# Gated linear attention inside a decoder layer: the coarsest level as a key-value state, two lanes of heads, tiles for pairs of heads

## The chip, the cores and the metric

One NeuronCore of a Trainium2 chip runs the whole program. The metric is the device time of one execution in microseconds; the kernel before took 889.64 us (median of 3 runs, 889.6 to 890.25). Engines are called as the profile calls them: PE is the matrix engine with its weight loads PEld, DVE the vector engine, ACT the scalar engine, POOL the general-purpose engine, SP the one that issues most loads.

## The reference

The reference is one decoder layer on 512 tokens of width 1024. A layer norm feeds one wide input projection, whose columns are split among gated linear attention (GLA, 4 heads, key width 128, value width 256), latent attention (MLA, 8 heads) and two branch gates. Both branches are projected back, merged by the gates, projected once more, normalised, and followed by a squared-ReLU MLP of width 4096. The part that is changed is GLA, which for each head computes

```
S_t = diag(a_t) S_{t-1} + k_t^T v_t
o_t = q_t S_t
```

with a decay a_t for every key channel, then a root-mean-square norm of o over its 256 columns, times silu(r), times an output projection:

```
log_a = log_sigmoid(a_lr @ w_gla_a2 + b_gla_a2) / 16
o_gla = gla_chunked(q * 128 ** -0.5, k, v, log_a)
y_gla = (rms_norm(o_gla) * silu(r_g)) @ w_o_gla
```

## The kernel before, in words

Everything is float32 in and out. Large products are made of three matmuls: each operand is split into a high part of type float32r and a low remainder (`split`, L104: one ACT copy for the high part, one DVE subtraction for the low one), and high x high, high x low and low x high are summed. Weights come through one list, `stream`; `pump` (L156) issues their loads on SP a few entries ahead and splits them (L179 on ACT, L180 on DVE) one entry ahead of their use.

**Lanes.** `gemm_tm` (tokens on the partitions) and `gemm_fm` (features on the partitions) run over the reduction in blocks of 128. After each block `tick` lets the first few generators of the list `active` (the first `WID[0]`) trace one step, up to their next `yield`. That is how small work is put between the matmuls of large products: a lane is a generator, and a step of it is what it does between two yields. A program then orders the instructions of each engine by a simulated timeline, with the order of tracing as priority.

**The stages around the change.** After the latents (`latents`, `latents2`) come the products of the input projection: queries, keys, then for each pair of heads `proj_v` and `proj_r` (values and output gates, 512 columns for two heads, 8 blocks each), then four products for the branch gates (`ev_g`, L941, tanh into the tiles `gt`) with the query-rope products `mla_qr` between them. GLA's levels and outputs run in lanes beside all of these; `finish(*t_gla)` (L972) closes the lanes ahead of `y_gla(0)`.

**Levels.** `gla_levels(h)` computes the 512x512 causal matrix of scores of a head by halves: at level s = 1, 2, 4, ..., 256 the right half of every block of 2s tokens looks at its left half, with decays taken relative to the middle. `advance` (L613, two POOL additions) keeps running sums of log decays in `rp`; `vec(s)` (L632) exponentiates them (ACT, L634) and multiplies them into queries and keys (DVE, L637 or L641) to give `M`; a matmul of the two halves of `M` gives the scores into a PSUM tile `px`; `take` (L646) puts them where they belong. Levels up to 64 go into the diagonal 128x128 blocks `SD` by a predicated copy; level 128 gives two blocks `s128`; level 256 gives, at L697, a 256x256 block of scores between the first and the last 256 tokens, as two matmuls with operands of type float32:

```
for j in range(2):
    mm(p[:, j * 256:(j + 1) * 256], M[:, j * P:(j + 1) * P], M[:, 256:], start=True, stop=True)
```

which `take` splits into `s256`. The first 256 columns of `M` are then the keys of the first half with their decays, the last 256 the queries of the last half with theirs. At the end the diagonal blocks are transposed where needed (L708) and split into `sd`. One lane, `lane_levels`, does the four heads one after the other.

**Outputs.** `gla_out(h)` waits until the levels, values and gates of its head are there, then sums for each block row i of 128 queries over its i + 1 blocks of keys (`blk`), three matmuls of 256 columns for each (L738 to L740), squares the result for the norm (L742), multiplies by the gate (`og`, L752), transposes (L758) and splits the result into `ogT` (L761). A lane of its own, `lane_out`, does this head after head.

**Buffers.** Tiles of tag A (24 buffers of 4 KB a partition) hold, among others, `latT`, `KK`, `qk`, `rp`, the values `vh` and `vl`, the gates `rg`, `sd`, `s256`, `ogT` and `gt`; tag B has 22 of 2 KB. PSUM has 4 banks for the large products (tag mm) and 4 for everything else (tag px). A tile waits until a buffer of its tag has been read for the last time. In `proj_v(1)` the evacuation is preceded by `levels_upto(1)`, which traces levels until heads 0 and 1 are through, so that their buffers are free.

Of the kernel before, what the change touches and what calls it, by code (L numbers as in the profile page):

```python
# [19 lines left out]
P = 128  # L20
# [32 lines left out]
def tile_hybrid_block(ctx: ExitStack, tc: tile.TileContext, I, out, dbg=None):  # L53
# [521 lines left out]
    Vh = [None] * GH  # L575
    Rg = [None] * GH
# [12 lines left out]
    def proj_r(hp):  # L589
        hs = (2 * hp, 2 * hp + 1)  # L590

        def e(a, j, ps):
            th = B([P, T], F32, "th")
            act(th, ps, AF.Tanh, scale=0.5)
            for i, h in enumerate(hs):
                if Rg[h] is None:
                    Rg[h] = A([P, NT, HV], F32, "rg")
                stt(Rg[h][:, a, :], th[:, i * HV:(i + 1) * HV], 1.0, ps[:, i * HV:(i + 1) * HV],
                    op0=ALU.add, op1=ALU.mult)
        gemm_tm([PL["r", hp]], hT, T, e)  # L600
# [3 lines left out]
    def gla_levels(h):  # L604
# [6 lines left out]
        s128 = s256 = None  # L611
# [34 lines left out]
        def take(s, p):  # L646
            nonlocal s128, s256
# [19 lines left out]
        advance(1)  # L667
        yield
# [16 lines left out]
        prev = None  # L685
        while s < T:
# [8 lines left out]
            else:  # L695
                for j in range(2):
                    mm(p[:, j * 256:(j + 1) * 256], M[:, j * P:(j + 1) * P], M[:, 256:], start=True, stop=True)  # L697
# [13 lines left out]
        take(*prev)  # L711
# [3 lines left out]
        SS[h] = (sd, s128, s256)  # L715
        yield

    def gla_out(h):
        while SS[h] is None or Vh[h] is None or Rg[h] is None:
            yield  # L720
        sd, s128, s256 = SS[h]

        def blk(j, i, w):
            if i == j:
                return sd[:, w, i, :]
            if j // 2 == i // 2:
                return s128[:, w, j // 2, :]
            return s256[:, w, j, (i - 2) * P:(i - 1) * P]

        vh, vl = Vh[h]  # L730
        ss = S([P, NT], F32, "gss")
        ps = []
        for i in range(NT):
# [3 lines left out]
            for j in range(i + 1):  # L737
                mm(o, blk(j, i, 0), vh[:, j, :], start=j == 0, stop=False)  # L738
                mm(o, blk(j, i, 0), vl[:, j, :], start=False, stop=False)
                mm(o, blk(j, i, 1), vh[:, j, :], start=False, stop=j == i)  # L740
# [9 lines left out]
        for i in range(NT):  # L750
            o = ps[i // 2][:, (i % 2) * HV:(i % 2 + 1) * HV]
            stt(og[i // 2][:, i % 2, :], o, rs[:, i:i + 1], Rg[h][:, i, :], op0=ALU.mult, op1=ALU.mult)  # L752
# [178 lines left out]
    t_gla = [t_lv, t_out]  # L931
# [376 lines left out]
```

## Time and profile before

| What | Value |
|---|---|
| median of 3 runs | 889.64 us (889.6 to 890.25) |
| the profiled execution | 889.94 us |
| its span, first to last instruction | 888.0 us |
| mean granted PE clock | 0.996 |
| input projection of values and gates, GLA, first branch gates | about 95 to 300 us of the span |
| HBM read, written | 82.56 MB, 3.67 MB |

Lines of the profile show a group of instructions as line, engine, operation, output tile <- input tiles, shapes, count, busy time, mean duration, and the idle time of the engine just before with what ended it. A piece of the chain has its start, its length and what it is; the chain is followed back from the last instruction, and a matmul's piece in it lasts until the next piece begins. Buffer numbers are left out of tile names, so `px` is any tile of tag px and `s` is `s128` or `s256`.

### The profile page before, as it was taken

The numbers are of one execution on the slowest core, as the hardware profiler recorded it, in microseconds if no ns is written. First come the engines' busy times: TensorE is split into PE (matmuls) and PEld (weight loads), VectorE is DVE, ScalarE is ACT, GpSimd is POOL, SyncE is SP. The second block draws the span as 40 slices with busy tenths as digits, with TensorE's granted clock in tenths as the row PEclk, the third lists the DMA queues.
The fourth block names the chain that finished last, engine by engine and source line by source line (L and its number), as shares of the span: only waits on it lengthen the run. The fifth ranks groups of instructions, "written<-read, shape, count | busy, mean of one in ns | idle before, by whom it ended". The sixth has DMA issues, their size and how long they took to land.

```text
span 888.0 us, 11561 instructions
## 1 busy us (share of the span) xinstructions
PE 866.7 (98%) x4352; PEld 738.3 (83%) x4352; DVE 578.2 (65%) x987; ACT 432.7 (49%) x734; POOL 173.8 (20%) x211
## 2 busy tenths in 40 slices
PE   5999999999999999999999999999999999999995
PEld 5988888888888888889888888988888888888884
DVE  7834875667735234657766797997557646754687
ACT  5446453445434334435654423466357546645661
POOL 0303441434512010000000012104400520242022
PEclk9999999999999999999999999999999999999998
DMA  7513223221223232111307628006940991398075
GB/s 231 147 48 90 77 72 95 72 72 48 78 59 88 74 107 91 61 46 55 102 25 277 190 70 286 1 0 158 296 117 25 258 254 31 70 308 192 1 189 95
DMA packets 63270, 101.13 MB, mean 114 GB/s; under 512 B 7761, under 2 KB 31748, under 8 KB 63216
## 3 DMA queue, kind: packets, MB, share of 16 engines
q1 hardware_dynamic: 48256, 64.04, 23.4%
q0 software_dynamic: 13040, 32.71, 15.3%
q10 hardware_dynamic: 1920, 3.66, 1.2%
q8 instruction: 34, 0.56, 0.2%
q14 instruction: 20, 0.16, 0.1%
HBM read 82.56 MB, written 3.67 MB: 97 GB/s over the span
## 4 chain that ended last, share of the span: by engine, by line
PE 95%; DVE 2%; DMA 2%; issue 1%; ACT 0%; POOLq 0%; SPq 0%; POOL 0%; DVEq 0%; ACTq 0%
PE mm L230 16%; PE mm L232 16%; PE mm L231 16%; PE mm L263 5%; PE mm L265 5%; PE mm L264 5%; PE px L1153 3%; PE px L1155 3%; PE px L1154 3%; PE mm L1153 2%; PE mm L1155 2%; PE mm L1154 2%; PE px L690 1%; DMA x<-in_x_dram 1%; PE px L852 1%; PE px L265 1%
## 5 line engine op out<-in xcount | busy, mean ns | idle before, releaser
L180 DVE TENSOR_TENSOR wlo<-wraw,whi 128x1024 fp32r<-128x1024 f32 (+1 forms) x104 | 117.4, 1129 | 152.8 <-ACT whi L179 147.6
L230 PE MATMUL mm<-h,whi 128*128 128x512 f32 x416 | 162.8, 393 | 0.0
L231 PE MATMUL mm<-h,whi 128*128 128x512 f32 x416 | 162.2, 390 | 0.0
L179 ACT ACTIVATE whi<-wraw 128x1024 fp32r<-128x1024 f32 (+1 forms) x104 | 100.2, 963 | 122.2 <-PE mm L231 62.9
L232 PE MATMUL mm<-h,wlo 128*128 128x512 f32 x416 | 155.3, 390 | 0.0
L1181 POOL DMA_DIRECT2D res<-ev x54 | 47.8, 989 | 236.2 <-ACT ev L1179 196.4
L232 PEld LDWEIGHTS mm<-h,wlo 128*128 128x128 f32 x416 | 78.1, 188 | 16.3
L230 PEld LDWEIGHTS mm<-h,whi 128*128 128x128 f32 x416 | 78.1, 188 | 15.6
L231 PEld LDWEIGHTS mm<-h,whi 128*128 128x128 f32 x416 | 78.1, 188 | 15.6
L264 PE MATMUL mm<-wlo,h 128*128 128x512 f32 x128 | 50.6, 395 | 0.0
L265 PE MATMUL mm<-whi,h 128*128 128x512 f32 x128 | 50.3, 394 | 0.0
L263 PE MATMUL mm<-whi,h 128*128 128x512 f32 x128 | 49.9, 400 | 0.0
L1235 ACT ACTIVATE relu<-mm 128x512 f32<-128x512 f32 x32 | 18.8, 595 | 57.3 <-PE mm L232 57.3
L351 POOL TENSOR_TENSOR mv<-mv,mhalf 128x1 f32<-128x1 f32 x4 | 5.5, 1385 | 209.2 <-DVE mv L350 209.2
L616 POOL TENSOR_TENSOR rp<-rp 128x256 f32<-128x256 f32 x32 | 29.9, 936 | 63.6 <-ACT E L634 52.8
L641 DVE TENSOR_TENSOR M<-E,qk 128x256 f32<-128x256 f32 x48 | 28.9, 629 | 12.4 <-ACT E L634 12.2
L634 ACT ACTIVATE E<-rp 128x512 f32<-128x512 f32 x32 | 20.4, 638 | 26.2 <-POOL rp L617 26.1
L179 ACT ACTIVATE xh<-wraw 128x1024 fp32r<-128x1024 f32 (+1 forms) x20 | 18.9, 959 | 26.9 <-PE mm L265 15.5
L180 DVE TENSOR_TENSOR wlo<-wq,whi 128x1024 fp32r<-128x1024 f32 x15 | 18.4, 1224 | 19.7 <-ACT whi L179 19.7
L265 PEld LDWEIGHTS mm<-whi,h 128*128 128x128 f32 x128 | 24.1, 188 | 4.8
L264 PEld LDWEIGHTS mm<-wlo,h 128*128 128x128 f32 x128 | 24.1, 188 | 4.5
L263 PEld LDWEIGHTS mm<-whi,h 128*128 128x128 f32 x128 | 24.0, 188 | 4.2
(381 smaller groups left out, 2235.2 us busy)
## 6 DMA issues: line engine op xcount, KB each, us to landing
wraw<-in_w_in_dram SPq DMA_DIRECT2D x40, 512.0 KB, 3.7
wraw<-in_w_ff_dram SPq DMA_DIRECT2D x32, 512.0 KB, 8.0
wq<-in_w_ff_dram POOLq DMA_DIRECT2D x32, 512.0 KB, 9.3
res<-ev POOLq DMA_DIRECT2D x54, 256.0 KB, 8.8
wraw<-in_w_o_gla_dram SPq DMA_DIRECT2D x8, 512.0 KB, 3.7
wraw<-in_w_o_mla_dram SPq DMA_DIRECT2D x8, 512.0 KB, 3.3
wraw<-in_w_out_dram SPq DMA_DIRECT2D x8, 512.0 KB, 4.2
wraw<-in_w_in_dram SPq DMA_DIRECT2D x8, 360.0 KB, 4.6
```

Source lines behind the costliest of these rows:

```text
L179: st["ins"] = act(hi[:, :nk, :n], raw[:, :nk, :n], AF.Copy)
L180: vtt(lo[:, :nk, :n], raw[:, :nk, :n], f(hi[:, :nk, :n]), op=ALU.subtract)
L230: mm(o, hi[:, c], xh, start=first, stop=False)
L231: mm(o, hi[:, c], xl, start=False, stop=False)
L232: mm(o, lo[:, c], xh, start=False, stop=last)
L263: mm(o, xh, hi[:, :n], start=opens, stop=False, skip_group_check=share)
L264: mm(o, xh, lo[:, :n], start=False, stop=False, skip_group_check=share)
L265: mm(o, xl, hi[:, :n], start=False, stop=last, skip_group_check=share)
L1153: mm(o, xh[:, c], hi[:, pp, cols], start=opens, stop=False, skip_group_check=True)
L1154: mm(o, xh[:, c], lo[:, pp, cols], start=False, stop=False, skip_group_check=True)
L1155: mm(o, xl[:, c], hi[:, pp, cols], start=False, stop=hf == 1 and pp == 1, skip_group_check=True)
L1181: nc.gpsimd.dma_start(res[tt + t][:, j * T:(j + 1) * T], e, accum_op=ALU.add)
```

## The change

Four things are changed, all in GLA.

1. Level 256 no longer makes scores. The keys' half of `M` is transposed on PE (two 128x128 transposes into `px`) and split into `kq[:, 0]`; the queries' half is split into `kq[:, 1]`. `gla_out` multiplies the transposed keys with the values of the first 256 tokens, which gives a state of 128x256 (6 matmuls), splits it into `sh` and `sl`, and for the block rows 2 and 3 multiplies the queries with this state, in place of two blocks of scores with their values.
2. Two lanes, `lane_levels(0)` and `lane_levels(1)`, do heads 0 and 2, and heads 1 and 3; the second starts one step later. Each level is two steps in place of one (matmul with the next level's `vec`, then `take`), with one more yield at the start and one after the first level. `WID[0]` is 4 in place of 3.
3. Values are split, and gates are made, in tiles of 2 token blocks x 512 columns for a pair of heads (`Vp`, `Rp`), in place of 4 blocks x 256 columns for each head (`Vh`, `Rg`); the number and the size of the tiles are the same.
4. `levels_upto(h)` steps the two lanes in turn.

```diff
     def proj_v(hp, guard=None):
-        hs = (2 * hp, 2 * hp + 1)
+        vp = []
         def e(a, j, ps):
-            for i, h in enumerate(hs):
-                if Vh[h] is None:
-                    Vh[h] = (A([P, NT, HV], F32R, "vh"), A([P, NT, HV], F32R, "vl"))
-                split(ps[:, i * HV:(i + 1) * HV], Vh[h][0][:, a, :], Vh[h][1][:, a, :])
+            if a % 2 == 0:
+                vp.append((A([P, 2, T], F32R, "vh"), A([P, 2, T], F32R, "vl")))
+            split(ps, vp[-1][0][:, a % 2, :], vp[-1][1][:, a % 2, :])
+            if a == NT - 1:
+                Vp[hp] = vp
...
     def proj_r(hp):
...
-            for i, h in enumerate(hs):
-                if Rg[h] is None:
-                    Rg[h] = A([P, NT, HV], F32, "rg")
-                stt(Rg[h][:, a, :], th[:, i * HV:(i + 1) * HV], 1.0, ps[:, i * HV:(i + 1) * HV],
-                    op0=ALU.add, op1=ALU.mult)
+            if a % 2 == 0:
+                rg.append(A([P, 2, T], F32, "rg"))
+            stt(rg[-1][:, a % 2, :], th, 1.0, ps, op0=ALU.add, op1=ALU.mult)
+            if a == NT - 1:
+                Rp[hp] = rg
...
         def take(s, p):
...
-                s256 = A([P, 2, 2, 2 * P], F32R, "s256")
-                split(p.rearrange("p (a b) -> p a b", b=256), s256[:, 0], s256[:, 1])
+                split(p[:, :256], kq[:, 0, 0], kq[:, 0, 1])
...
         advance(1)
         yield
+        yield
...
-        prev = None
+        yield
         while s < T:
...
                 for j in range(2):
-                    mm(p[:, j * 256:(j + 1) * 256], M[:, j * P:(j + 1) * P], M[:, 256:], start=True, stop=True)
-            if prev is not None:
-                take(*prev)
-            prev = (s, p)
+                    nc.tensor.transpose(p[:, j * P:(j + 1) * P], M[:, j * P:(j + 1) * P], ident)
+                kq = A([P, 2, 2, 256], F32R, "kq")
+                split(M[:, 256:], kq[:, 1, 0], kq[:, 1, 1])
+            if 2 * s < T:
+                M = vec(2 * s)
+            yield
+            take(s, p)
             s *= 2
             if s < T:
-                M = vec(s)
-            yield
+                yield
...
     def gla_out(h):
...
+        def V(j):
+            c = slice(h % 2 * HV, (h % 2 + 1) * HV)
+            return [t[:, j % 2, c] for t in Vp[h // 2][j // 2]]
+        p = PX()[:, :HV]
+        for j in range(2):
+            vh, vl = V(j)
+            kh, kl = [kq[:, 0, w, j * P:(j + 1) * P] for w in range(2)]
+            mm(p, kh, vh, start=j == 0, stop=False)
+            mm(p, kh, vl, start=False, stop=False)
+            mm(p, kl, vh, start=False, stop=j == 1)
+        sh, sl = B([P, HV], F32R, "gst"), B([P, HV], F32R, "gst")
+        split(p, sh, sl)
...
-            for j in range(i + 1):
-                mm(o, blk(j, i, 0), vh[:, j, :], start=j == 0, stop=False)
-                mm(o, blk(j, i, 0), vl[:, j, :], start=False, stop=False)
-                mm(o, blk(j, i, 1), vh[:, j, :], start=False, stop=j == i)
+            todo = [(sd[:, 0, i, :], sd[:, 1, i, :], *V(i))]
+            if i % 2:
+                todo.append((s128[:, 0, i // 2, :], s128[:, 1, i // 2, :], *V(i - 1)))
+            if i > 1:
+                c = slice((i - 2) * P, (i - 1) * P)
+                todo.append((kq[:, 1, 0, c], kq[:, 1, 1, c], sh, sl))
+            for n, (ah, al, bh, bl) in enumerate(todo):
+                mm(o, ah, bh, start=n == 0, stop=False)
+                mm(o, ah, bl, start=False, stop=False)
+                mm(o, al, bh, start=False, stop=n == len(todo) - 1)
...
-    def lane_levels():
-        for o in range(2):
-            nc.vector.tensor_copy(lmask[:, :, o], lmi[:, o, :, None, :].to_broadcast([P, len(LEVELS), 2, 64]))
-        for h in range(GH):
+    def lane_levels(first):
+        if first == 0:
+            for o in range(2):
+                nc.vector.tensor_copy(lmask[:, :, o], lmi[:, o, :, None, :].to_broadcast([P, len(LEVELS), 2, 64]))
+        else:
+            yield
+        for h in range(first, GH, 2):
             yield from gla_levels(h)
             lv[h] = True
...
-    t_lv, t_out = spawn(lane_levels()), spawn(lane_out())
+    t_lv, t_out = [spawn(lane_levels(first)) for first in range(2)], spawn(lane_out())
     def levels_upto(h):
-        while not lv[h]:
-            step(t_lv)
-    WID[0] = 3
+        for g in range(h + 1):
+            while not lv[g]:
+                step(t_lv[g % 2])
+    WID[0] = 4
```

More of the change, by code (lines that the diff above doesn't have):

```diff
@@ L610, in gla_levels @@
         SD = B([P, NT, P], F32, "SD")
-        s128 = s256 = None
+        s128 = kq = None
         def advance(s):
@@ L646, in take @@
         def take(s, p):
-            nonlocal s128, s256
+            nonlocal s128, kq
             if s <= 64:
@@ L710, in gla_levels @@
         gtt(sd[:, 1, :2], SD[:, :2], f(sd[:, 0, :2]), op=ALU.subtract)
-        take(*prev)
         yield
@@ L714, in gla_levels @@
         split(pt, sd[:, 0, 2:], sd[:, 1, 2:])
-        SS[h] = (sd, s128, s256)
+        SS[h] = (sd, s128, kq)
         yield
     def gla_out(h):
-        while SS[h] is None or Vh[h] is None or Rg[h] is None:
+        while SS[h] is None or Vp[h // 2] is None or Rp[h // 2] is None:
             yield
[L721 to L730, printed above, removed]
+        sd, s128, kq = SS[h]
+        def V(j):
[10 more added lines that the diff above has]
+        split(p, sh, sl)
         ss = S([P, NT], F32, "gss")
@@ L751, in gla_out @@
             o = ps[i // 2][:, (i % 2) * HV:(i % 2 + 1) * HV]
[L752 removed]
+            stt(og[i // 2][:, i % 2, :], o, rs[:, i:i + 1], Rp[h // 2][i // 2][:, i % 2, h % 2 * HV:(h % 2 + 1) * HV],
+                op0=ALU.mult, op1=ALU.mult)
         yield
@@ L930, in tile_hybrid_block @@
     proj_r(1)
-    t_gla = [t_lv, t_out]
+    t_gla = [*t_lv, t_out]
     gt = [None] * NK
```

6 lines of the change are left out of this document (3 added, 3 removed).

## The prediction

> **What bounds the kernel now.** First the page: busy shares, then the chain that ended last.
>
> ```profile
> span 888.0 us, 11561 instructions
> ...
> PE 866.7 (98%) x4352; PEld 738.3 (83%) x4352; DVE 578.2 (65%) x987; ACT 432.7 (49%) x734; POOL 173.8 (20%) x211
> ...
> PE 95%; DVE 2%; DMA 2%; issue 1%; ACT 0%; POOLq 0%; SPq 0%; POOL 0%; DVEq 0%; ACTq 0%
> ```
>
> TensorE is busy for 98% of the span and makes up 95% of the chain. That is an average, so the next view is the busy time in the stretch where the changed code runs (the four value and gate projections and the first branch-gate products, 95 to 300 us) and in the three that follow; columns are busy time and instructions of PE, weight loads, DVE, ACT, POOL, then granted clock, DMA share, GB/s. From the list of the weight loads' waits over the whole run stands the one row of a late weight split (total, times, longest).
>
> ```profile
> 95.00:300.00 205.00, 204.95 (x1079) 175.43 (x1078) 129.54 (x245) 95.41 (x182) 70.41 (x86) 1.00 0.26 75
> 300.00:400.00 100.00, 99.49 (x510) 84.15 (x509) 46.86 (x97) 36.78 (x69) 4.01 (x4) 1.00 0.24 72
> 400.00:500.00 100.00, 99.97 (x555) 87.15 (x554) 69.59 (x172) 54.22 (x117) 0.00 (x0) 1.00 0.37 125
> 500.00:600.00 100.00, 99.65 (x545) 86.19 (x544) 89.96 (x137) 42.11 (x64) 11.33 (x12) 1.00 0.30 98
> ```
> ```profile
> PEld mm L232 <- DVE wlo L180: 0.9, 1, 0.9
> ```
>
> In the changed stretch PE stands still for 0.05 us of 205, at full clock, while DVE is busy 63% and ACT 47%. So two things decide: what the edit does to the sum of PE's own time, which falls through to the end, and whether the new order opens holes in a stream that has none. Time on ACT, DVE and POOL costs nothing until it makes PE wait. A busy PE need not be PE at its peak, so the prices come from the chain, where each piece lasts until the next begins.
>
> **The PE terms.** Pieces of heads 0 and 1 from the chain (start, us, what), then the groups of the stretch, which give the counts (busy, mean ns; that mean overlaps with its neighbours and is no price).
>
> ```profile
> 127.38 0.22 PE px L708 x2
> ```
> ```profile
> 174.76 0.86 PE px L697 x4
> 175.62 0.44 PE px L758 x4
> ...
> 180.18 0.12 PE px L738
> ```
> ```profile
> L738 PE MATMUL px<-vh,s 128*128 128x256 f32 x24 | 7.0, 293 | 0.0
> L758 PE MATMUL px<-ca,og 128*128 128x128 f32 x32 | 5.0, 272 | 0.0
> L738 PE MATMUL px<-vh,sd 128*128 128x256 f32 x16 | 4.7, 296 | 0.0
> L697 PE MATMUL px<-M 128*128 128x256 f32 x16 | 4.1, 379 | 0.0
> L708 PE MATMUL px<-ca,SD 128*128 128x128 f32 x8 | 1.5, 272 | 0.0
> ```
>
> *Removed*: the level-256 score block, two float32 matmuls of 256 columns per head at L697. They stand as 16 records for four heads, so two for each matmul: 4 records, 0.86 us per head, 3.44 us in all.
>
> *Added in its place*: two transposes of 128x128 float32 per head. Transposes show one record each (8 at L708 for four heads' two, 32 at L758 for four heads' eight), 0.22 us for two in the one row and 0.44 for four in the other. So 0.22 us per head, 0.88 in all.
>
> *Output products*: before, head h has 1+2+3+4 = 10 blocks of three matmuls of 256 columns, which is the 24 + 16 = 40 of L738 over four heads. After: three each for block rows 0 to 3 with 1, 2, 2 and 3 blocks, that is 8 blocks, and 2 more for the state, 10 again. Thirty matmuls per head at 0.12 us before and after: nothing gained, nothing lost. What looks like the point of the change, a smaller product, is an equal one here; the gain sits in the float32 scores.
>
> Sum on PE: 0.88 - 3.44 = -2.56 us. Bounds for the transposes, which run before this in other places only: by L708 and L758 0.11 each; if they cost what a float32 matmul of 128 columns does, half of an L697 matmul (0.86 / 2 / 2 = 0.215), 0.43 per head and the sum is -1.72. I take 0.11: same operation, same type, same shape as in those two rows.
>
> The Trainium skill, page "TensorE: Matmul & The Clock Gate", Part 4 (PE-mode transpose), gives about 275 ns for a transpose inside a kernel. The two groups of transposes above agree with it as a duration (272 ns), but their spacing in the chain is 0.11 us; by 275 ns each, one after the other, the estimate of the sum would be 4 x 0.55 - 3.44 = -1.24 us.
>
> **ACT and DVE.** The rows for the tiles that become wider, and for their neighbours of the other width:
>
> ```profile
> L107 DVE TENSOR_TENSOR vl<-mm,vh 128x256 fp32r<-128x256 f32 x16 | 6.0, 413 | 0.1
> L598 DVE SCALAR_TENSOR_TENSOR rg<-th,mm 128x256 f32<-128x256 f32 x16 | 5.7, 414 | 1.7 <-ACT th L594 1.7
> L107 DVE TENSOR_TENSOR s<-px,s 128x512 fp32r<-128x512 f32 x4 | 2.7, 678 | 0.0
> L106 ACT ACTIVATE vh<-mm 128x256 fp32r<-128x256 f32 x16 | 5.6, 399 | 0.4 <-PE mm L265 0.2 <-DVE vl L107 0.2
> L106 ACT ACTIVATE s<-px 128x512 fp32r<-128x512 f32 x4 | 2.5, 614 | 0.6 <-PE px L697 0.6
> ```
>
> Value and gate tiles of 512 columns: 16 x 0.413 becomes 8 x 0.678 on DVE (-1.2 us), the same for the gate product at L598 (16 x 0.414 to 8 x 0.68, -1.2), and 16 x 0.399 to 8 x 0.614 on ACT (-1.5). Level 256: one split of 512 columns per head becomes three of 256 (keys, scaled queries, state): ACT 4 x (3 x 0.399 - 0.614) = +2.3, DVE 4 x (3 x 0.413 - 0.678) = +2.2. Net +0.8 us on ACT and -0.2 on DVE over 205 us: nothing, covered by PE's stream. The state's split is the one new wait inside a chain: its two instructions (0.40 + 0.41 us) stand between the state's last matmul and the third block row's second product; the first two block rows (9 matmuls, 1.1 us) and a step of the projection lie between. No DMA is added or moved.
>
> **The two lanes.** One round of a projection is 12 matmuls of 512 columns (4 x 0.68 = 2.7 us of PE), after which every lane takes one step. These are the stations of one level:
>
> ```profile
> L641 DVE TENSOR_TENSOR M<-E,qk 128x256 f32<-128x256 f32 x48 | 28.9, 629 | 12.4 <-ACT E L634 12.2
> L634 ACT ACTIVATE E<-rp 128x512 f32<-128x512 f32 x32 | 20.4, 638 | 26.2 <-POOL rp L617 26.1
> ...
> L616 POOL TENSOR_TENSOR rp<-rp 128x256 f32<-128x256 f32 x32 | 29.9, 936 | 63.6 <-ACT E L634 52.8
> L617 POOL TENSOR_TENSOR rp<-rp 128x256 f32<-128x256 f32 x32 | 24.0, 750 | 9.7 <-ACT q L660 7.5
> ```
>
> 0.94 + 0.75 + 0.64 + 2 x 0.63 = 3.6 us for one level, against one step of 2.7 before and two (5.4) after. Each head gets slower, but two run at once. Counting yields: a head takes 12 steps before and 21 after, so four heads take 48 and then 43 (the second lane starts one later). Work per step rises by 48/43, 12%; DVE's 63% in the stretch has room. I cost it at nothing. If that cover goes, the weight split L180 is late, and PE stands.
>
> What follows the levels has slack too: the last head's transposes L758 stand at 272.73 (next fence), and the branch-gate products that must come before their use end at 319.0. In steps, the last output starts about three later than before (49 against 46, 8 us), of 46 us.
>
> **Sum.** The profiled execution took 889.94 us (span 888.0), 0.30 over the median of the runs, 889.64. 889.94 - 2.56 = 887.4, and **887.1** for the median: 0.29% faster. A measurement of this kernel tells about 0.2%, 1.78 us, from no change.
>
> **Rivals.** The rows for them: the tanh of the second branch-gate product and where it waits (ACT, in time; an execution row's last bracket is the idle time before it and its releaser), head 3's output products (PE), all of L941, and two chain pieces.
>
> ```profile
> 264.99 2.03 ACT L941 ACTIVATE gt<-mm,hbg 128x512 f32<-128x512 f32 x3
> ...
> 267.73 0.69 ACT L941 ACTIVATE gt<-mm,hbg 128x512 f32<-128x512 f32 x1 [0.40 <-PE px L740]
> ```
> ```profile
> 259.17 0.28 PE L738 MATMUL px<-vh,sd 128*128 128x256 f32 x1
> ...
> 268.12 0.28 PE L740 MATMUL px<-vh,sd 128*128 128x256 f32 x1
> ```
> ```profile
> L941 ACT ACTIVATE gt<-mm,hbg x16: 672/690/694, 238.1 to 319.0; 128x512 f32<-128x512 f32 x16
> ```
> ```profile
> 272.73 0.87 PE px L758 x8
> ...
> 323.27 1.14 DVE wlo L180
> ```
>
> *A. The buffers run out (slower).* The 24 buffers of tag A hold latents, keys, values, gates, levels' results, outputs and branch gates. Before, at the second branch-gate product, 25 are asked for (6 latents and rope keys, 3 values and gates of head 3, its 2 level results, 6 outputs, 4 + 4 branch gates), and the trace shows it: the fourth tanh sits idle for 0.40 us until an L740 product of head 3 is done. After, values and gates are held by pairs until the second head is through, and head 3's output starts later: 6 + 4 + 2 + 2 + 4 outputs + 4 + 4 = 26. Two tiles wait, and behind them ACT's queue and the two accumulators that the next gate product needs. For: the row. Against: the query-rope product (36 matmuls of 0.12 us) lies before that next product, needs other accumulators, and PE executes head 3's first block rows, which free two buffers, in it. At the second value projection the count is 24, full but not over. Price if the cover fails: head 3's products take from 259.17 to 268.24 (the last one's start + 0.12), 9.1 us with 3.6 of PE's own; PE stands for at most 5.5. Then 887.1 + 5.5 = 892.6, slower by 0.33%. It decides from 4.3 us of new standstill (2.56 + 1.78).
>
> *B. Small holes take the gain back (no measurable change).* Late weight splits: one occurs already, the 0.9 us wait on L180, which stood behind other DVE work at 323.27 and left PE idle 0.51 us between 300 and 400. With 12% denser vector work ahead of the split, one such hole at each of the four projections' ends is 4 x 0.5 = 2.0: 889.1. For: DVE is the busiest of the others. Against: evacuations get shorter by the widths above, and 0.05 us of idle in 205 leaves little sign that the queue is near its limit.
>
> *C. The transposes cost more (no measurable change).* At 272 ns in a row, the groups' mean, 4 x 2 x 0.272 = 2.18 in place of 3.44 gives -1.26: 888.4. Against it the spacing of 0.11 in both rows. At 0.215 it is 887.9, on the edge. The skill's figure on that page would give the same result, since it is the duration.
>
> *D. More than the sum.* Existing holes may close as the order shifts: 0.05 + 0.51 + 0.03 + 0.35 = 0.94 between 95 and 600. That bounds a surplus: 886.1.
>
> **Chances.** Forecast, with new holes under 0.8 us: 0.60, its own range 886.1 to 887.9. D 0.03. B 0.20, C 0.05. A 0.12. Faster is forecast and D, 0.63; same is B and C, 0.25; slower is A, 0.12. Range: from 885.9, just under D's bound, up to 890.4, which takes in C and holes of up to 3.3 us; most of A and little else is left out.
>
> **What would show it.** In the trace after: no L697-like matmul of 256 columns, and two transpose records there, 0.22 us apart from their follower; 32 records at each of the three output lines and 8 at each of the state's three; PE's busy time between 95 us and the end of the branch-gate products shorter by 2.5 us at equal idle; the tanh of gate tiles idle on an output product, by how much longer than 0.40 tells A's size. If PE shows waits of over 1 us in the list between 95 and 330, or transposes spaced at more than 0.15, the sum is wrong; if the stretch gains 2.5 us and the end does not, it was given back behind it, in the attention stage.

## The result and the profile after

The changed kernel takes **898.2 us** (median of 5 runs, 897.59 to 899.05) against 890.25 (5 runs, 889.6 to 890.9): a ratio of 1.0084, interval 1.0070 to 1.0099. It was forecast at 887.1 with 885.9 to 890.4 as the range; it became slower by 8 us. The profiled execution took 897.59 us, its span is 895.5, 7.5 more than before.

The page after, span, busy shares and the chain that ended last:

```profile
span 895.5 us, 11522 instructions
...
PE 867.9 (97%) x4344; PEld 738.6 (82%) x4344; DVE 583.3 (65%) x979; ACT 434.3 (49%) x734; POOL 169.6 (19%) x211
...
PE 90%; DVE 6%; DMA 2%; issue 1%; ACT 1%; POOLq 0%; POOL 0%; SPq 0%; DVEq 0%; ACTq 0%
```

The shares hardly moved, but DVE went from 2% to 6% of the chain. The next view is the busy time of the stretch from 95 to 300 us and of the three behind it (columns as in the prediction), then the list of what PE waited for between 95 and 330 us (total, times, longest).

```profile
95.00:300.00 205.00, 198.69 (x1038) 169.46 (x1037) 132.61 (x235) 93.33 (x177) 66.11 (x85) 0.98 0.25 72
300.00:400.00 100.00, 99.49 (x503) 83.90 (x502) 43.88 (x91) 35.98 (x67) 3.90 (x4) 1.00 0.24 71
400.00:500.00 100.00, 99.97 (x561) 87.39 (x559) 70.15 (x176) 55.52 (x122) 0.00 (x0) 1.00 0.34 113
500.00:600.00 100.00, 99.65 (x544) 86.19 (x543) 89.19 (x132) 39.79 (x58) 11.21 (x12) 1.00 0.35 116
```
```profile
PE px L691 <- DVE SD L651: 3.0, 1, 3.0
PE px L691 <- DVE M L642: 2.4, 1, 2.4
PE mm L263 <- DVE vl L107: 0.5, 1, 0.5
PE px L675 <- DVE SD L684: 0.4, 1, 0.4
```

All of the loss is in the changed stretch: PE stands for 205 - 198.69 = 6.31 us there (0.05 before), at a granted clock of 0.98, and for as long as before in the three others. Two waits of level matmuls (L691) on DVE make up 5.4 us of it (the first two rows). Here is the first, on PE, at the end of the first value projection (start, duration, instruction; in brackets the idle time before it and its releaser):

```profile
123.35 0.39 PE L265 MATMUL mm<-whi,h 128*128 128x512 f32 x1
123.58 1.50 PE L691 MATMUL px<-M 128*128 128x128 f32 x12
128.09 1.22 PE L691 MATMUL px<-M 128*128 128x128 f32 x4 [3.01 <-DVE SD L651]
129.86 0.79 PE L263 MATMUL mm<-whi,h 128*128 128x512 f32 x1 [0.55 <-DVE vl L107]
130.45 0.63 PE L264 MATMUL mm<-wlo,h 128*128 128x512 f32 x1
...
134.59 0.39 PE L265 MATMUL mm<-whi,h 128*128 128x512 f32 x1
```

The last matmul of the product starts at 123.35. Level matmuls follow that need no more than what DVE has delivered; then PE stands, and the next product cannot begin because its accumulators are still to be evacuated (L107). When it does begin, its matmuls of 512 columns have 0.63 us in place of 0.39: the clock record of the trace grants 0.5 from 127.6 to 134.4 us. What DVE, and POOL beside it, did meanwhile:

```profile
123.40 1.25 DVE L180 TENSOR_TENSOR wlo<-wraw,whi 128x1024 fp32r<-128x1024 f32 x1
124.57 3.12 DVE L642 TENSOR_TENSOR M<-E,qk 128x256 f32<-128x256 f32 x4
127.61 0.42 DVE L651 COPY_PREDICATED SD<-cmask,px 128x256 f32<-128x256 uint8 x1
127.94 1.26 DVE L642 TENSOR_TENSOR M<-E,qk 128x256 f32<-128x256 f32 x2
129.13 0.68 DVE L107 TENSOR_TENSOR vl<-mm,vh 128x512 fp32r<-128x512 f32 x1
129.73 0.74 DVE L642 TENSOR_TENSOR M<-E,qk 128x256 f32<-128x256 f32 x2
```
```profile
128.13 0.79 POOL L617 TENSOR_TENSOR rp<-rp 128x256 f32<-128x256 f32 x1
129.00 0.68 POOL L618 TENSOR_TENSOR rp<-rp 128x256 f32<-128x256 f32 x1
```

DVE has no pause: a weight split of 1.25 us, then four level products in a row (the same level of both lanes), a masked copy and two more products, and only at 129.13 the evacuation. Two more things are to be seen. DVE was late long before the hole; the chain, which before runs on PE alone between 100 and 130 us, now runs mostly on DVE there, in pieces like these:

```profile
116.22 2.32 DVE M L642 x4
...
118.80 2.45 DVE M L642 x3
```

And its products are slow while POOL adds: four take 3.12 us (0.78 each) beside POOL's additions, two take 0.74 (0.37 each) right after the last of them has ended at 129.68.

The busy time of 110 to 135 us, before and then after, says how full DVE was (the same columns):

```profile
110.00:135.00 25.00, 25.00 (x127) 21.06 (x126) 18.64 (x34) 13.17 (x27) 10.94 (x15) 1.00 0.21 64
```
```profile
110.00:135.00 25.00, 21.08 (x95) 17.38 (x94) 25.00 (x42) 10.85 (x18) 18.82 (x23) 0.86 0.15 43
```

18.64 of 25 us became 25.00 of 25, and POOL went from 10.94 to 18.82. The second hole, 2.4 us at the end of the second gate projection (215 us), has another shape: DVE had an idle moment just before it, and the product that PE waits for stands behind a weight split, one small instruction and two masked copies in DVE's order.

```profile
214.92 1.23 DVE L180 TENSOR_TENSOR wlo<-wraw,whi 128x1024 fp32r<-128x1024 f32 x1 [0.42 <-ACT whi L179]
216.06 0.61 DVE L757 TENSOR_SCALAR gss<-gss 128x4 f32<-128x4 f32 x1
216.59 0.75 DVE L651 COPY_PREDICATED SD<-cmask,px 128x256 f32<-128x256 uint8 x2
217.25 0.75 DVE L642 TENSOR_TENSOR M<-E,qk 128x256 f32<-128x256 f32 x2
217.92 2.47 DVE L598 SCALAR_TENSOR_TENSOR rg<-th,mm 128x512 f32<-128x512 f32 x4
```

So the time is accounted for: 6.26 us more of standstill, and some 2.9 us for the half clock (an estimate: in the 6.8 us of half clock PE worked 5.8, and half of that is lost; 2.2 of it because eleven matmuls of 512 columns came every 0.43 us instead of 0.23). That leaves, by difference, about 1.7 us of PE work saved: 6.3 + 2.9 - 1.7 = 7.5. What had to be settled is which part of the change opens such holes, and whether the saving is there at all.

### The profile page after: what moved, and what is told of

Its sections match the earlier page's. It is cut to its first block, busy times and chain, and to the rows that moved or that the text cites. A ratio compares the mean times of both kernels' runs of the same rounds, so it can differ in the third digit from the quotient of the medians.

```text
span 895.5 us, 11522 instructions
## 1 busy us (share of the span) xinstructions
PE 867.9 (97%) x4344; PEld 738.6 (82%) x4344; DVE 583.3 (65%) x979; ACT 434.3 (49%) x734; POOL 169.6 (19%) x211
## 4 chain that ended last, share of the span: by engine, by line
PE 90%; DVE 6%; DMA 2%; issue 1%; ACT 1%; POOLq 0%; POOL 0%; SPq 0%; DVEq 0%; ACTq 0%
PE mm L230 16%; PE mm L232 16%; PE mm L231 16%; PE mm L263 5%; PE mm L265 5%; PE mm L264 5%; PE px L1170 3%; PE px L1172 3%; PE px L1171 3%; PE mm L1172 2%; PE mm L1170 2%; PE mm L1171 2%; DVE M L642 2%; DMA x<-in_x_dram 1%; PE px L865 1%
## 5 line engine op out<-in xcount | busy, mean ns | idle before, releaser
L180 DVE TENSOR_TENSOR wlo<-wraw,whi 128x1024 fp32r<-128x1024 f32 (+1 forms) x104 | 117.7, 1133 | 158.2 <-ACT whi L179 147.5
L642 DVE TENSOR_TENSOR M<-E,qk 128x256 f32<-128x256 f32 x48 | 31.3, 693 | 1.8 <-ACT E L635 1.8
L180 DVE TENSOR_TENSOR wlo<-wq,whi 128x1024 fp32r<-128x1024 f32 x15 | 18.4, 1223 | 19.7 <-ACT whi L179 19.7
```

The lines of the kernel that those rows point to most:

```text
L180: vtt(lo[:, :nk, :n], raw[:, :nk, :n], f(hi[:, :nk, :n]), op=ALU.subtract)
L642: vtt(packed(M, s, i), pairs(E[:, 2 * i * P:2 * (i + 1) * P], s), half_lr(qk, s, i), op=ALU.mult)
```

## The experiments

Times are medians, ratios are against the kernel before on the same chip, with their interval. "Standstill" is 205 us less PE's busy time from 95 to 300 us. A "hole" is counted from the start of PE's last matmul ahead of it to the start of the next one, so it is longer than the wait in the profile's list by the 0.27 to 0.42 us of that matmul (3.28 us here for the first wait of 3.0, 2.66 for the second of 2.4). "Phase" is where the steps of the levels fall against the ends of the products.

### Each part alone

Three kernels made from the one before by one part of the diff each, and one with two parts: the key-value state (e1), the two lanes (e2), the pair tiles (e3), state and tiles in one lane (e4). The letters in the expectations name the suspects: L is the two lanes, S the state, T the tiles. The edits are those of the diff above; e1, for instance:

```diff
-                    mm(p[:, j * 256:(j + 1) * 256], M[:, j * P:(j + 1) * P], M[:, 256:], start=True, stop=True)
+                    nc.tensor.transpose(p[:, j * P:(j + 1) * P], M[:, j * P:(j + 1) * P], ident)
+                kq = A([P, 2, 2, 256], F32R, "kq")
+                split(M[:, 256:], kq[:, 1, 0], kq[:, 1, 1])
...
```

> The kernel before with the key-value state alone: one lane of levels, values and gates per head. Theory L (two lanes put more vector work into one projection than DVE can do, PE stands behind it): no holes over 1 us, the float32 scores are gone, so 2.6 us under the kernel before, between 1.6 and 3.4. Theory S (the state's transposes, splits and its wait are what costs): 4 us or more over the kernel before. Theory T (512-column evacuations are late): as L, since the tiles are not in it.

> The kernel before with the two lanes and their step structure alone: scores at level 256, values and gates per head. Theory L: the holes of the changed kernel come back without the state, so its loss without its gain, 8 + 2.6 = about 10 us over the kernel before, between 6 and 13, with a hole of 2 us or more near the end of the first value projection and PE at half clock behind it. Theories S and T: within 1.5 us of the kernel before.

> The kernel before with values and gates in tiles for pairs of heads alone. Theory T: 4 us or more over the kernel before, with DVE's low parts of the values late at the end of the first value projection. Theories L and S: within 1.5 us of the kernel before; shorter evacuations (some 1 us on each of DVE and ACT) give PE nothing, since it does not wait for them.

> The changed kernel with the lanes taken back: state and pair tiles stay, one lane, one step per level. Theory L: 2.6 us under the kernel before, between 1.6 and 3.6, as the sum of the prediction has it. Theories S and T: still over the kernel before by 3 us or more.

| kernel | us | ratio | standstill, us | holes over 2 us, at |
|---|---|---|---|---|
| e1, state | 894.92 | 1.0049 (1.0036 to 1.0062) | 4.47 | 3.06 at 211 |
| e2, lanes | 898.25 | 1.0085 (1.0072 to 1.0098) | 5.15 | 3.27 at 124, 2.08 at 128 |
| e3, tiles | 897.82 | 1.0079 (1.0067 to 1.0091) | 4.15 | 2.98 at 212 |
| e4, state and tiles | 898.75 | 1.0090 (1.0076 to 1.0103) | 6.17 | 2.33 at 206, 2.71 at 210 |

Each of the three parts alone makes the kernel slower, by 4.5 to 7.9 us (state and tiles together by 8.4), and the three losses sum to far more than the whole change lost. Theory L foretold e2, with its hole and the half clock behind it, but a gain for e1 and e4; S and T foretold the losses of e1 and e3, and T had the hole of e3 at another place. So no one part is guilty, and the price is not the price of an operation. Two shapes can be told apart. With two lanes (e2 here, from 110 to 135 us) DVE is as full as in the changed kernel:

```profile
110.00:135.00 25.00, 20.17 (x95) 17.27 (x96) 25.00 (x46) 10.53 (x21) 18.17 (x22) 0.86 0.20 56
```

With one lane DVE is hardly fuller in that stretch than before (e1 18.74, e3 19.51, e4 18.60 us, before 18.64), PE does not stand there, and the holes over 2 us are near the end of the second gate projection. In e3, which changes nothing but the tiles, DVE starts the level-256 product that PE waits for at 213.97, behind a weight split (211.51) and two output splits (212.65).

### Level matmuls held behind the product

Rival: PE's fixed order has level matmuls too early, ahead of work that it could do. f1 (the changed kernel), f2 (e4) and f10 (e1) put each of them behind the latest matmul of the large product:

```diff
-                    mm(o, xl, hi[:, :n], start=False, stop=last, skip_group_check=share)
+                    st["mm"] = mm(o, xl, hi[:, :n], start=False, stop=last, skip_group_check=share)
...
+        def lmm(op, *a, **kw):
+            with tc.issue_after(st["mm"].ins):
+                op(*a, **kw)
...
-                    mm(p[:, u * P:(u + 1) * P], M[:, 0, u, :], M[:, 1, u, :], start=True, stop=True)
+                    lmm(mm, p[:, u * P:(u + 1) * P], M[:, 0, u, :], M[:, 1, u, :], start=True, stop=True)
```

> The changed kernel with one addition: every matmul and transpose of the levels is issued on PE behind the last matmul of a large product that was traced ahead of it, so none can be put ahead of the next product's first matmuls. Theory O (PE's fixed order holds level matmuls at the end of a product, and PE stands there until DVE has made their operands): the waits of 3.0 and 2.4 us on level matmuls are gone, and the time falls from 898 to 887 to 889. Theory D (DVE itself is behind in the first projection, whatever PE's order): the wait moves to the next product's first matmul, which waits for the low part of the values, 2 us or more there, 892 to 897.

> State and pair tiles in one lane, as before, with the same addition. Theory O: the waits of 4.4 us on level matmuls near the end of the second gate projection go, 887 to 889.5. Theory D: DVE is at 60% in that stretch, so it has no say here; if the time stays over 894, theory O is wrong for one lane.

> The key-value state alone in one lane (895 without the addition), with the level matmuls behind the large product's. Theory O: the 2.8 us wait on a level matmul and its half clock go, 887 to 889.5. If it stays at 893 or more, the state itself costs.

f1 took 901.25 us (ratio 1.0124, 1.0108 to 1.0139), f2 898.31 (1.0093, 1.0079 to 1.0107), f10 896.61 (1.0070, 1.0058 to 1.0083): none better than its kernel without the edit by more than 0.5 us. The waits of PE in f1:

```profile
PE mm L263 <- DVE vl L107: 5.7, 1, 5.7
PE mm L230 <- DVE rg L598: 2.9, 1, 2.9
```

The level matmuls no longer wait at these ends, and the next product's first matmul waits in their place, for the evacuations, longer than before. At these ends it is DVE that is late, and which of PE's matmuls stands first does not help. In f2 and f10 the hold did not move the hole at all: PE still waits for level products, 4.3 us against 4.4 in e4 and 3.2 against 3.2 in e1. So for kernels with one lane these two leave the rival undecided.

### The same instructions, one empty step earlier or later

If the fixed order on DVE at the ends decides, then the phase of the level steps against the products must do so too, with no work changed. f4 is the kernel **before** with one empty step ahead of the levels:

```diff
     def lane_levels():
...
+        yield
         for h in range(GH):
             yield from gla_levels(h)
```

> The kernel before with one empty step ahead of the levels: the same instructions on every engine, every level traced one step later. Theory O says that what decides is where the levels' steps fall against the products' ends, so this alone moves the time by 2 us or more, most likely up, 892 to 898. If only added or removed work matters, it stays within 1 us of the kernel before.

900.5 us, ratio 1.0117 (1.0103 to 1.0131): 10.4 us for an empty step. PE's waits between 95 and 330 us, and the hole, which stands behind the two transposes of one head and ahead of the next head's first level:

```profile
PE px L674 <- ACT vh L106: 3.7, 1, 3.7
PE px L697 <- DVE M L637: 2.2, 1, 2.2
```
```profile
178.33 0.38 PE L708 MATMUL px<-ca,SD 128*128 128x128 f32 x2
182.45 2.90 PE L674 MATMUL px<-x,qk 128*128 128x192 f32 x8 [3.74 <-ACT vh L106]
```

In the kernel before the same two follow one another without a wait. The larger wait is put down to ACT and not to DVE. The copies L664, which the next head's first level needs, start on ACT at 180.88, behind evacuations of the values and a weight split, and in the kernel before at 177.32 (f4 first, then before):

```profile
180.88 0.45 ACT L664 ACTIVATE x<-qk 128x256 f32<-128x256 f32 x1
```
```profile
177.32 0.73 ACT L664 ACTIVATE x<-qk 128x256 f32<-128x256 f32 x2
```

So either engine's fixed order can open such a hole. This settles most of it: the kernel before sits in a phase in which no such meeting occurs, and it loses more by leaving it than the changed kernel lost. The next two move kernels that have the change, by two steps (the levels of each lane behind two empty steps):

```diff
+        for _ in range(2):
+            yield
         for h in range(first, GH, 2):
```

> The kernel before with the key-value state alone, and two empty steps ahead of the levels, which moves all of them by two rounds of a product against its end; the instructions are the same as without the empty steps (894.92 us). Theory P (the phase of the levels against the ends decides): the time differs by more than 2 us from 894.92, with the holes in other places; a phase without holes gives 887 to 888. Rival (the state itself costs time): 894 to 896 us, the hole near 211 us stays.

> The changed kernel with two empty steps ahead of each lane of levels, the instructions the same. Theory P: the time differs by more than 2 us from 898.2, holes in other places; a phase without holes gives 887 to 888. Rival (two lanes and pair tiles cost their time at any phase): 897 to 900 us with the holes at 125 and 215 us.

g2 (e1 and two steps) took 903.35 us (1.0144, 1.0129 to 1.0159), 8.4 more than e1, with a standstill of 9.53 us: four holes of 1.2 to 2.4 us between 176 and 187 us, where e1 has one of 1.4, and the one at the end of the second gate product still there, 2.44 us in place of 3.06. g4 (the changed kernel and two steps) took **891.33** (1.0014, 1.0005 to 1.0024), 6.9 less than the changed kernel, with 3.38 us of standstill and full clock in the whole stretch. The program's instructions are the same within each of the three pairs (with f4 and the kernel before); the phase is worth -7 to +10 us. DVE is full in g4 too, 10.00 of 10 us from 120 to 130, and the hole there is only 1.04 us: what counts is what stands on a full DVE at the end of a product. That a phase without any hole would be met so easily was too hopeful.

### Keeping the levels in step

f5 (the changed kernel) and f11 (e1) place each level's exponential behind the latest weight split's instruction on ACT, so that the levels cannot run ahead of the products:

```diff
-            act(pairs(E, s), lr(rp, s), AF.Exp, scale=1.0 / 16.0)
+            with tc.issue_after(st["ins"].ins):
+                act(pairs(E, s), lr(rp, s), AF.Exp, scale=1.0 / 16.0)
```

> The changed kernel, with the exponential of each level placed behind the latest weight split's instruction on ACT, so that levels keep step with the products; all work is kept. Theory D (at the end of a product the vector engine has level work in its fixed order that it ran too early or too late, and TensorE stands behind it): with levels paced there is less vector work bunched at the ends, the two holes of 3.3 and 2.7 us and the half clock after the first go, 888 to 893 us. Rival (the place of the levels in the order decides and pacing only moves it): a hole of 2.5 us or more is again at an end of a value or gate product, 895 to 901 us.

> The kernel before with the key-value state alone, and the same pacing of the levels; all work is kept. Theory D: the hole of 3.06 us at 211 us and the half clock behind it go, and the 2.56 us of TensorE show: 887 to 890 us. Rival (place decides): 893 to 898 us with a hole of 2.5 us or more at an end.

f5: 893.21 us (1.0039, 1.0021 to 1.0057). Its stretch from 110 to 135 us:

```profile
110.00:135.00 25.00, 24.66 (x125) 21.01 (x125) 20.92 (x34) 10.01 (x16) 11.43 (x13) 1.00 0.22 64
```

DVE falls from 25.00 to 20.92 us there, POOL from 18.82 to 11.43, and the first hole is gone: the third of a microsecond that is left is an earlier wait, at 110 us, which the changed kernel has too (0.4 us, the last row of its list). So that hole came from bunched vector work, though pacing also shifts the order. The second stays at 2.66 us. f11: 895.39 (1.0056, 1.0041 to 1.0071), the hole of 3.06 us unmoved, as the rival said; it fits that in one lane nothing was bunched that pacing could spread.

### Fewer level steps at the ends

h9 is e1 with the levels not stepped in the round before the last of each value and gate product.

```diff
+    def tick(width, quiet=False):
         for g in list(active[:width or WID[0]]):
-            step(g)
+            if not (quiet and g in levels):
+                step(g)
...
-                tick(width)
+                tick(width, k == nk - 2)
```

> The kernel before with the key-value state alone (894.92 us), and the levels not stepped in the one round before the last of each value and gate product, so that less level work stands at their ends; all work is kept. Theory P: the hole of 3.06 us at the end of the second gate product shrinks below 1.5 us, no half clock follows, 888 to 891. Rival (what is not done at the end is done in a lump elsewhere): a hole of 2.5 us or more remains, 893 us or more.

900.17 us (1.0108, 1.0089 to 1.0128), far outside what theory P expected. The hole at that end shrank, from 3.06 to 1.85 us, but everything behind the first skipped step had a new phase, and at the end of the second value projection 1.17, 2.39, 1.51 and 2.48 us appeared between 175 and 186 us.

### Towards a phase without holes

> The changed kernel with both edits that helped alone: the levels' exponential behind the latest weight split (893.21 alone) and two empty steps ahead of each lane (891.33 alone); all work is kept. Theory P (only the meeting of level work with the ends of the products costs time): holes of less than 2 us in all between 95 and 300 us and the time at 887.5 to 889.5. Rival (each edit moves the order anew and their gains do not add): a hole of 2 us or more, 891 to 897.

> The changed kernel with the exponential behind the weight split, and one empty step between the two heads of each lane, which moves only the second pair of heads. The one large hole of the version without the empty step (2.66 us at 208 us, behind it 3.5 us of half clock; 893.21 us) lies in the second pair. Theory P: it changes by over 1 us with the rest as it was, 888 to 890 if it goes. Rival: it stays at 2.4 to 2.9 us, 892 to 894.

> The changed kernel with two empty steps ahead of each lane (891.33 us) and one more between the two heads of each lane. Of its holes over 0.7 us (1.04 at 124, 2.03 at 208, 0.94 at 272) only the last two can move. Theory P: the hole at 208 us changes; without it and without a new one 888.5 to 889.5. Rival: 891 to 892, the hole stays.

h1 joins the two edits that helped: **890.42 us** (0.9997, 0.9988 to 1.0007), no change against before. i2 (pacing, one empty step between a lane's two heads) took 892.69 (1.0023, 1.0014 to 1.0033): the hole of the second pair stayed at 2.66 us although all its levels were traced a step later, as the rival said, so one step is not enough to know where a hole goes. i4 (two steps, and one between the heads) took 894.62 (1.0047, 1.0031 to 1.0064): the hole at 208 us went, as theory P said, and one of 3.03 us came at 269, where the first matmul of a gate product waits for the rotation of the rope queries (L447) on DVE; neither expectation had that.

In h1 two holes over 0.7 us were left in the stretch. At the larger, DVE runs the two lanes' products in a row (its timeline):

```profile
207.39 2.78 DVE L643 TENSOR_TENSOR M<-E,qk 128x256 f32<-128x256 f32 x4
...
210.43 1.86 DVE L598 SCALAR_TENSOR_TENSOR rg<-th,mm 128x512 f32<-128x512 f32 x3
```

The last two kernels are h1 with one lane shifted against the other there, by an empty step between the two heads of the second lane (j_lane1_1) or of the first (j_lane0_1):

```diff
             lv[h] = True
+            for _ in range(1 * (first == 1)):
+                yield
```

> The changed kernel with the paced exponential and two empty steps ahead (890.42 us; holes of 1.54 us at 207 and 0.94 at 271), and one empty step between the two heads of the second lane alone, so that the two lanes' products of the second pair no longer meet in the same steps: at the hole, four of them (2.78 us) stand in a row on the vector engine. All work is kept. Theory P: the hole at 207 us goes or halves, 888.5 to 889.8, faster than the kernel before. Rival (another meeting takes its place): 890 us or more, with a hole of 1 us or more between 170 and 300 us.

> The same with the empty step between the two heads of the first lane alone. Theory P: as the other, 888.5 to 889.8 if the hole at 207 us goes. Rival: 890 us or more, with a hole of 1 us or more between 170 and 300 us. Where one of the two lanes is a step late and the other is not, the two results may differ by more than 1 us though the instructions are the same: that too speaks for the phase.

j_lane1_1 took **889.36 us** (11 runs, 888.41 to 890.01) against 890.01 (21 runs): 0.9989, 0.9980 to 0.9998, a little faster than the kernel before. Of the nine kernels that have all of the change it is the only one that is faster, and only by 0.65 us. j_lane0_1 took 891.52 (1.0016, 1.0007 to 1.0025), with holes of 1.05, 0.85 and 1.19 us at 201, 269 and 272 us. DVE at the place in j_lane1_1, and PE's waits from 95 to 330 us:

```profile
207.26 1.21 DVE L643 TENSOR_TENSOR M<-E,qk 128x256 f32<-128x256 f32 x2 [0.75 <-ACT E L636]
...
208.73 1.87 DVE L598 SCALAR_TENSOR_TENSOR rg<-th,mm 128x512 f32<-128x512 f32 x3
```
```profile
PE mm L230 <- ACT gt L963: 0.7, 1, 0.7
PE mm L232 <- DVE wlo L180: 0.5, 1, 0.5
PE px L751 <- ACT osq L755: 0.3, 1, 0.3
```

Two products instead of four stand ahead of the evacuation L598, which starts at 208.73 and not at 210.43, and of the hole a wait of 0.3 us is left (L751).

### What the runs say together

Four kernels have all of the change and full clock through the stretch. The rows of the stretch in g4, h1, j_lane1_1 and j_lane0_1, in this order:

```profile
95.00:300.00 205.00, 201.62 (x1065) 172.47 (x1064) 129.86 (x222) 96.14 (x180) 64.73 (x80) 1.00 0.26 75
```
```profile
95.00:300.00 205.00, 202.80 (x1071) 173.72 (x1070) 134.29 (x224) 96.01 (x180) 67.16 (x80) 1.00 0.27 77
```
```profile
95.00:300.00 205.00, 203.91 (x1076) 174.63 (x1075) 132.80 (x224) 96.16 (x180) 68.60 (x80) 1.00 0.27 77
```
```profile
95.00:300.00 205.00, 202.42 (x1065) 172.45 (x1064) 131.65 (x223) 95.29 (x180) 69.22 (x80) 1.00 0.27 75
```

In these single profiled executions, span less standstill is 889.1 - 3.38 = 885.7, 888.1 - 2.20 = 885.9, 886.8 - 1.09 = 885.7 and 888.8 - 2.58 = 886.2; before, 888.0 - 0.05 = 887.95. So without its holes the change takes 1.7 to 2.2 us off, and what decides between 889 and 898 is the standstill and the half clock that long holes bring.

## Why the prediction was wrong, step by step

**The PE terms** were right in kind and nearly in size. In the profile after there are eight transposes (L698), a pair of them 0.38 us long in the timeline, so 0.11 us apart, and no level-256 score matmul of M with M; the state's products have 8 records at each line, as counted:

```profile
L698 PE MATMUL px<-ca,M 128*128 128x128 f32 x8 | 1.5, 272 | 0.0
L732 PE MATMUL px<-vh,kq 128*128 128x256 f32 x8 | 2.5, 311 | 0.0
```

Forecast -2.56 us; the four kernels without half clock show -1.7 to -2.2, and PE's busy time on their pages, 864.5, 864.2, 864.6 and 865.1 against 866.7, shows -1.6 to -2.5. What the missing 0.4 to 0.9 us are was not tried. In the four traces, from the start of each matmul to the next and without the standstill, the 112 remaining level records of M with M take 11.3 to 11.7 us, 10.5 before; the sum held them unchanged. And the removed ones took 3.1 us by this count, not 3.44. Rival C's transposes of 272 ns in a row did not happen.

**The two lanes** are the step that failed, in its words "DVE's 63% in the stretch has room. I cost it at nothing." The lanes alone (e2) cost 7.9 us, and in the changed kernel the first hole with its half clock is theirs, as e2 and f5 show: 3.6 of the 6.3 us of standstill and all of the half clock. The 63% were the mean of 205 us. The stretch from 110 to 135 us had 18.64 of 25 us on DVE already, 75%, and the second lane filled it to 25.00. Even the 75% was flattering: it holds a pause of 4.57 us from 130 us on, and from 105 to 130 us DVE had 22.93 of 25 us before. The cover was used up there, and the sentence behind it came true, but at another instruction: not the weight split L180 was late, the evacuation and the level products behind that split were. The prices of the stations were taken from means as well: 0.63 us for a product is a mean over products beside POOL's additions and products without them, and where two lanes keep POOL adding, each takes about 0.78. In the group, 48 products went from 28.9 to 31.3 us:

```profile
L642 DVE TENSOR_TENSOR M<-E,qk 128x256 f32<-128x256 f32 x48 | 31.3, 693 | 1.8 <-ACT E L635 1.8
```

**What no step asked** was where in the products' rounds the level steps fall. The prediction counted yields (12, 21, 48, 43) for length only. e3 and f4 show what that is worth: tiles that were to take work off ACT and DVE cost 7.4 us (897.82 against 890.38), an empty step 10.4, about as much as the whole change (8 us) or more. "0.05 us of idle in 205 leaves little sign that the queue is near its limit" was the wrong reading: it was the sign of an order in which the ends happened to be free. DVE's own mean cannot show it, since the hole at 215 us came in a place where DVE had just been idle.

**The rivals.** B had the right mechanism, vector work ahead of a split at the projections' ends, but four holes of 0.5 us were its price and there were two waits of 3.0 and 2.4, and behind the longer one the half clock, which no rival had. A did not occur in the changed kernel: no tanh of a gate tile there makes PE wait. It does occur in h1, where the tanh (ACT) is released by an output product:

```profile
270.91 1.26 ACT L961 ACTIVATE gt<-mm,hbg 128x512 f32<-128x512 f32 x2 [0.26 <-PE px L752]
```

PE's wait on gt is 0.7 us there and in g4, i2 and j_lane1_1 (its list above), against up to 5.5 in A. D did not occur.

**The test named beforehand**, PE waits of over 1 us between 95 and 330 us, was the right one and gave the answer at once.

Shown is that the phase decides, with the instructions held fixed (f4, g2, g4), that two lanes fill DVE at the first pair of heads (e2, and f5, which undoes it), and that a version nearly without holes (1.09 us of standstill) is faster than the kernel before, by 0.65 us (j_lane1_1). Not shown is why the order on DVE comes out as it does at an end, and no run could say beforehand in which phase a hole appears (theory P failed in i2 and h9). That the slower products beside POOL make DVE late at the first hole is argued from its rows; the additions were not moved to another engine.

## What to carry to other kernels

Where PE has no standstill, read the cover from the stretch of some 25 us in which the new work lands, without the pauses at its edges, and from the queue of DVE at the end of each product, not from a mean over the stage; a saving of 0.3% on the bound engine is smaller than what a shift by one or two steps can be worth (here -7 to +10 us). Before an edit of a stepped schedule is judged, run it in a few phases, with empty steps, and run the old kernel in them too: both the loss of the change and the speed of the kernel before were in large part their phase (for the kernel before one other phase was run, f4). To compare work, take the standstill off the spans first.

## What the runs showed of the hardware

A standstill of 3 us costs more than itself. At or behind the holes the clock record grants 0.5 for 6.8 us (the changed kernel, 3.28 and 0.97 us of hole; f4, 4.01) or for 3.4 (e1, 3.06; f5, 2.66; f4's second, 2.45), but it does not do so for the 2.03 us of g4, nor for the 2.66 us in the changed kernel at 215 us. In the traces of all runs every stretch on the record but the last, at 1.0 or at 0.5, lasts a whole number of steps of 3.41 us. The Trainium skill, page "TensorE: Matmul & The Clock Gate", Part 1, has the clock drop to half after an idle window of about 3.4 us that runs freely, not from the start of the standstill; the steps of 3.41 us and the 0.5 of one or two of them agree with that, while holes shorter than 3.4 us were enough here, as 2.66 and 2.45 us show, and a hole of the same length may or may not do it. The ten runs of f5, one program, fit this: their mean granted clock goes from 0.992 to 0.997 and their time from 899.09 to 891.57 us.

Products of two SBUF operands on DVE take nearly twice as long beside additions of POOL: of the 48 in the changed kernel, the 35 that run beside POOL's work for at least nine tenths of their time take 0.75 us on average and the four beside an idle POOL 0.41. The 35 are not alike, though: single ones take from 0.41 to 1.09 us, and seven of them no more than 0.46. The Trainium skill, page "SBUF — State Buffer", section "Who interferes with whom", has a DVE instruction with two SBUF inputs contend with a GpSimd (POOL) instruction that reads SBUF, over a shared pair of ports that it calls an exclusive lock. The slowdown agrees with a shared port. If every product waited for one whole addition of 0.68 us it would take 0.41 + 0.68 = 1.09 us (an estimate from these rows), and four took 3.12 us with POOL adding end to end; how the two engines take turns stays open.
